# The state-space branch of a transformer kernel without GpSimd, and the attention's lambda at the very start

## The chip, the cores and the metric

The kernel runs on one core of a Trainium2 chip. A core has a matrix engine, TensorE (PE; its weight loads are listed apart as PEld), and three engines for elementwise work: VectorE (DVE), ScalarE (ACT) and GpSimd (POOL). Transfers are issued from the queues of SyncE (SP) or of another engine. Each engine takes its instructions in order, and waits on semaphores for the others. The metric is the device time of one execution in microseconds (us), as the median of several runs. In the profile L178 is line 178 of the kernel.

## The reference

One block over 512 tokens of width 1024: a state-space branch and a differential attention side by side, merged through gates, then cross attention to a memory, a feed-forward part, and two more layers with four branches each. The change touches only the first part:

```python
def s5_branch(u, lam_re, lam_im, log_dt, b_re, b_im, c_re, c_im, d_skip):
    ...
    lam_bar = jnp.exp(lam * dt)
    b_bar = ((lam_bar - 1.0) / lam)[..., None] * b
    bu = jnp.einsum('gph,blgh->lbgp', b_bar, ug)
    ...
    _, states = lax.associative_scan(combine, (a, bu), axis=0)
    y = jnp.einsum('ghp,lbgp->blgh', c, states).real
    y = y.reshape(bsz, seqlen, SSM_WIDTH) + d_skip.astype(F32) * u.astype(F32)
```

It has 64 groups of 16 channels with 64 complex states each. The differential attention (8 heads) subtracts a second softmax from a first, scaled by one number: lambda = exp(q1·k1) − exp(q2·k2) + a constant, from four learned vectors of 64 elements.

## The kernel before

**Matmuls.** Products in full precision are made from halves: each matrix is split into a rounded part and a remainder, and three matmuls are summed. A weight comes by transfer into a tile `raw`; ACT writes the rounded part `wh` (L177), DVE the remainder `wl` (L178); PE then runs `L1415` or `L272` matmuls of 128x512. Activations are split in the same way (`ap`, `qk`, `vv` and others).

**The mix stage.** `mix()` fills the first 480 us or so and is followed by cross attention, feed-forward and the other layers, which the change doesn't touch. It has four phases. (1) Four tiles of the input are normalised (`norm_tile`: ACT sums squares at L219, DVE makes the inverse root at L206 to L214, POOL or DVE scales at L296) and transposed. The first two weights of the state-space input are rounded by POOL (L1026). (2) The matmuls of u (`u_mm`, L272 and L1035), beside them `ssm_prep()`, which turns lambda and the step size into powers, and the first steps of the state-space generator. (3) The attention `da()`: per head and row block scores, softmax, the weights' combination (L894 to L897), output (L914), and a norm row (L925 to L928). A generator `fill()` puts the projections of later heads (`qk_in`, with the rotary step L960 to L967) and the gates between them. (4) The gated unit `glu()`, which reads the state-space output back from memory (`ysd`).

**The state-space generator.** `ssm_half(sp, hf, ...)` is run for two halves of 32 groups. It makes factors (L570 to L579) and a table of powers `apw` (L584 to L590); 16 pieces z of 128x512, three POOL instructions each (L608 to L610), which PE transposes (L614), ACT copies (L616) and PE multiplies with u (L623) into the state `E`; a scan in two levels of seven steps, k (L637 to L641) and b (L646 to L650), whose real part is on POOL and whose imaginary part is on DVE; then 16 pieces W of 128x576, again three POOL instructions each (L684 to L686), and the output (L717 to L741). Over both halves that makes 16 z and 16 W pieces. Each `yield` ends a step. In phase 2 the table `U_STEPS` sets how many steps follow each u tile; in phase 3 the attention earns a credit of 2.5 steps per turn (`SSM_RATE`).

**Order.** The kernel is written in the Tile framework: dependencies become semaphores, and a scheduler orders the instructions of each engine, starting from the order of the code.

**Lambda.** `da_lambda()` (L855 to L876) loads the four vectors into one partition of a tile `rp`, forms the two sums and exponentials on DVE (`exp_acc`, L411 to L423) and spreads the result over 128 partitions by a matmul with ones (L874). It is called after the last u matmul and before `fill()` begins:

```python
        p = self.psum("tp")
        nc.tensor.matmul(p[:, 0:2], z[0:1, 128:256], z[0:1, 16:18], start=True, stop=True)
        self.nlam = self.cst.tile([128, 1], F32, name="nlam")
        v.tensor_copy(self.nlam, p[:, 0:1])
```

Of the kernel before, what the change touches and what calls it, by code (L numbers as in the profile page):

```python
# [119 lines left out]
class Builder:  # L120
# [231 lines left out]
    def load_cols(self):  # L352
# [43 lines left out]
        nc.vector.tensor_scalar(self.half_glu, self.col("b_glu"), 0.5, None, op0=OP.mult)  # L396
        self.onesr = self.cst.tile([128, 1], F32R, name="onesr")
        nc.vector.tensor_scalar(self.onesr, self.ident[:, 0:1], 0.0, 1.0, op0=OP.mult, op1=OP.add)
# [61 lines left out]


    def ssm_prep(self, sp):
        nc, A, v = self.nc, self.A, self.nc.vector
        tl = lambda name, w: sp.tile([128, w], F32, name=name)
        k = [0]
# [11 lines left out]
        lr, li, dt, ld = new(), new(), new(), new()
        nc.sync.dma_start(lr, A["ssm_lambda_re"][0])
        nc.sync.dma_start(li, A["ssm_lambda_im"][0])
        nc.sync.dma_start(ld[:, 0:1], A["ssm_log_dt"][0].rearrange("(g o) -> g o", o=1))  # L480
        self.exp_acc(dt[:, 0:1], ld[:, 0:1], lambda: new()[:, 0:1])
# [55 lines left out]
        p1, p2 = tl("p1", 576), tl("p2", 576)  # L537
        v.tensor_copy(p1[0:64], pr[0:64])
        v.tensor_copy(p1[64:128], pi[64:128])
        v.tensor_copy(p2[0:64], pi[0:64])  # L540
        v.tensor_copy(p2[64:128], pr[64:128])
        self.P1, self.P2 = (x.rearrange("p (k g) -> p k g", k=9) for x in (p1, p2))
        asc = tl("asc", 128).rearrange("p (q f l) -> p q f l", q=4, f=8)
        for h in range(2):
            s = slice(h * 64, h * 64 + 64)
            for q, z in ((0, prv), (1, prv), (3, piv)):
                zz = z[s, 0].rearrange("p (f h l) -> p f h l", f=8, h=2)[:, :, h]
                v.tensor_copy(asc[s, q], zz)
        v.tensor_scalar(asc[:, 2], asc[:, 3], -1.0, None, op0=OP.mult)
        self.asc = asc.rearrange("p q f l -> p q (f l)")  # L550

    def ssm_half(self, sp, hf, us, ys, kd):
        nc, A, v, G = self.nc, self.A, self.nc.vector, self.nc.gpsimd
        g0 = hf * 32
# [14 lines left out]
        tmp = spg()  # L569
        G.tensor_mul(v3(B1), v3(U), bc(self.Frd))  # L570
        G.tensor_mul(v3(tmp), v3(V), bc(self.Fis))
        G.tensor_add(B1, B1, tmp)
        tmp = spg()
        G.tensor_mul(v3(X2), v3(V), bc(self.Frs))
        G.tensor_mul(v3(tmp), v3(U), bc(self.Fid))
        G.tensor_sub(X2, X2, tmp)
        v.tensor_copy(X1[0:64], B1[0:64])
        v.tensor_copy(X1[64:128], X2[64:128])
        v.tensor_copy(X2[64:128], B1[64:128])  # L579

        a = self.asc[:, :, hf * 16:hf * 16 + 16]
        ap = tl(384, "apw", 1).rearrange("p (q g k) -> p q g k", q=3, g=16)
        ct = self.small(64, "ct4", 1).rearrange("p (g k) -> p g k", g=16)
        v.tensor_copy(ap[:, 0, :, 0:1], a[:, 0, :, None])  # L584
        v.tensor_copy(ap[:, 1, :, 0:1], a[:, 3, :, None])
        for n in (1, 2, 4):
            m = ap[:, :, :, n - 1:n].to_broadcast([128, 3, 16, n])
            self.cmul(v, ap[:, 0, :, n:2 * n], ap[:, 1, :, n:2 * n], ap[:, 0, :, 0:n], ap[:, 1, :, 0:n],
                      m[:, 0], m[:, 1], ct[:, :, 0:n])
        v.tensor_scalar(ap[:, 2], ap[:, 1], -1.0, None, op0=OP.mult)  # L590
        yield
# [4 lines left out]
        for fl in range(4):  # L596
            u = self.page()
            nc.sync.dma_start(u, us[hf * 4 + fl])
            us_.append(u.rearrange("p (g c) -> p g c", g=8))
            Rs = []  # L600
            for h in range(2):
                gl = fl * 8 + h * 4
                z, t2 = spg(), spg()
                zv, tv = (x.rearrange("p (g k h) -> p g k h", g=4, k=8) for x in (z, t2))
                pw = lambda P: P[:, 1:9, g0 + gl:g0 + gl + 4].rearrange("p k g -> p g k")[
                    :, :, :, None].to_broadcast([128, 4, 8, 16])
                bw = lambda B: v3(B)[:, gl:gl + 4, None, :].to_broadcast([128, 4, 8, 16])
                G.tensor_mul(zv, pw(self.P1), bw(X1))  # L608
                G.tensor_mul(tv, pw(self.P2), bw(X2))
                G.tensor_add(z, z, t2)  # L610
                yield
                tp = self.psum("sx")
                for g in range(4):
                    nc.tensor.transpose(tp[:, g * 128:g * 128 + 128], z[:, g * 128:g * 128 + 128], self.ident)  # L614
                R = self.page()
                nc.scalar.activation(R, tp, AF.Copy)  # L616
                Rs.append(R)
                yield
            xp = self.psum("sx").rearrange("p (r l c) -> p r l c", r=2, l=4)
# [14 lines left out]
        for k in range(1, 8):  # L634
            pr = Eb[:, :, :, :, k - 1]
            for r, e in enumerate((G, v)):
                e.tensor_mul(m1[:, r], ab(0), pr[:, r])  # L637
                e.tensor_mul(m2[:, r], ab(2 + r), pr[:, 1 - r])
                e.tensor_add(m1[:, r], m1[:, r], m2[:, r])
            for r, e in enumerate((G, v)):  # L640
                e.tensor_add(Eb[:, r, :, :, k], Eb[:, r, :, :, k], m1[:, r])  # L641
            yield
        for b in range(1, 8):
            cr = lambda r: Eb[:, r, :, b - 1, 7:8].to_broadcast([128, 16, 8])
            for r, e in enumerate((G, v)):
                e.tensor_mul(m1[:, r], ap[:, 0], cr(r))  # L646
                e.tensor_mul(m2[:, r], ap[:, 2 - r], cr(1 - r))
                e.tensor_add(m1[:, r], m1[:, r], m2[:, r])
            for r, e in enumerate((G, v)):
                e.tensor_add(Eb[:, r, :, b, :], Eb[:, r, :, b, :], m1[:, r])  # L650
            yield
# [8 lines left out]
        for dst, key, sg in ((C1, "ssm_c_re", True), (C2, "ssm_c_im", False)):  # L660
# [5 lines left out]
            for f in range(4):  # L666
                nc.tensor.transpose(tp[:, f * 128:f * 128 + 128], ci[:, f * 128:f * 128 + 128], self.ident)
            if sg:
                v.tensor_scalar(dst, tp, self.sgn, -1.0, op0=OP.mult, op1=OP.mult)
            else:  # L670
                v.tensor_scalar(dst, tp, -1.0, None, op0=OP.mult)
            yield
# [3 lines left out]
        def kern(n):  # L676
# [175 lines left out]
    def da_lambda(self):  # L852
        nc, A, v = self.nc, self.A, self.nc.vector
        r = self.page(tag="rp")
        for j, n in enumerate(("da_lambda_q1", "da_lambda_k1", "da_lambda_q2", "da_lambda_k2")):  # L855
            nc.sync.dma_start(r[0:1, j * 64:j * 64 + 64], A[n])
        rv = r[0:1, 0:256].rearrange("p (a b n) -> p a b n", a=2, b=2)
# [12 lines left out]
        v.tensor_scalar(z[0:1, 16:17], z[0:1, 16:17], LAM_INIT, -1.0, op0=OP.add, op1=OP.mult)  # L870
        v.memset(z[0:1, 128:256], 1.0)
        v.tensor_copy(z[0:1, 17:18], z[0:1, 16:17])
        p = self.psum("tp")
        nc.tensor.matmul(p[:, 0:2], z[0:1, 128:256], z[0:1, 16:18], start=True, stop=True)  # L874
        self.nlam = self.cst.tile([128, 1], F32, name="nlam")
        v.tensor_copy(self.nlam, p[:, 0:1])  # L876

    def da(self, qk, need, vgen, yad, ssd, mask):
# [5 lines left out]
        def start(u):  # L884
# [37 lines left out]
        def norm(h, sq):  # L922
# [47 lines left out]
    def mix(self, stage=5):  # L970
# [82 lines left out]
        for f in range(8):  # L1053
# [962 lines left out]
```

## Time and profile before

| | |
|---|---|
| median of 3 runs | 2199.04 us (2193.31 to 2204.34) |
| the profiled execution | 2190.39 us |
| its span in the profile | 2188.4 us |
| mean granted PE clock | 0.979 |
| PE busy | 2094.1 us (96%) |
| DVE busy | 1301.3 us (59%) |
| ACT busy | 984.9 us (45%) |
| POOL busy | 350.6 us (16%) |

Busy times are sums over the whole span. The mix stage is about a fifth of it, and the shares there are others than these. The last matmul's end sets the end of the span, so the time that PE stands still, or runs at the lower clock, is what a change of the other engines can win or lose.

### The profile page before, as it was taken

What the parts mean: (1) busy time and instruction counts of PE and PEld (TensorE: products, weight loads), DVE (VectorE), ACT (ScalarE), POOL (GpSimd) and SP (SyncE); (2) the same over time, 40 slices, a digit from 0 to 9 for tenths busy, and PEclk for the clock granted to TensorE, in tenths of its full rate; (3) what the DMA queues carried; (4) which work ended last, traced back from release to release, by engine and by line L of the source; (5) the groups of instructions that cost most, each with busy time, mean ns of one, the idle gap of its engine ahead of it and who ended that gap; (6) DMA issues with size and microseconds to landing.
All of it is one profiled execution on the core that took longest, in us unless ns stands there. A gap on an engine that the chain in (4) does not pass through costs nothing.

```text
span 2188.4 us, 29605 instructions
## 1 busy us (share of the span) xinstructions
PE 2094.1 (96%) x11102; PEld 1729.9 (79%) x11102; DVE 1301.3 (59%) x2935; ACT 984.9 (45%) x1945; POOL 350.6 (16%) x310
## 2 busy tenths in 40 slices
PE   6798998989999999999999999999999999999998
PEld 6576776767788988888888887888888887888886
DVE  7788579655557556233336767674345667674344
ACT  5255664654247446342334645453234545453232
POOL 2676389400010000000001000001210000001210
PEclk8899999999999999999999999999999999999999
DMA  6424523445633331222233323232234323232321
GB/s 173 123 79 118 132 83 87 137 132 195 212 117 126 116 97 58 97 96 96 80 113 118 121 69 99 68 110 92 89 104 141 102 63 112 73 106 87 106 98 66
DMA packets 244614, 234.93 MB, mean 107 GB/s; under 512 B 56264, under 2 KB 198255, under 8 KB 244471
## 3 DMA queue, kind: packets, MB, share of 16 engines
q1 hardware_dynamic: 244470, 233.04, 34.5%
q8 instruction: 87, 1.43, 0.3%
q14 instruction: 57, 0.46, 0.1%
HBM read 212.01 MB, written 18.91 MB: 106 GB/s over the span
## 4 chain that ended last, share of the span: by engine, by line
PE 80%; DVE 10%; DMA 3%; ACT 3%; issue 2%; POOL 1%; SPq 0%; DVEq 0%; ACTq 0%; POOLq 0%
PE mm L1415 39%; PE mm L282 18%; PE mm L272 13%; DVE wl L178 2%; DMA rp<-rsd 1%; PE o L1681 1%; PE mm L1099 1%; PE sx L717 1%; PE at L842 1%; PE at L843 1%; DMA raw<-in_w_in 1%; PE o L1490 1%; ACT wh L177 1%; PE at L1291 1%; PE o L1329 1%
## 5 line engine op out<-in xcount | busy, mean ns | idle before, releaser
L178 DVE TENSOR_TENSOR wl<-raw,wh 128x1024 fp32r<-128x1024 f32 (+1 forms) x310 | 402.1, 1299 | 384.4 <-ACT wh L177 380.7
L177 ACT ACTIVATE wh<-raw 128x1024 fp32r<-128x1024 f32 (+1 forms) x310 | 332.3, 1074 | 466.9 <-PE mm L1415 177.4
L1415 PE MATMUL mm<-pg,wh 128*128 128x512 f32 (+1 forms) x896 | 276.4, 388 | 14.0 <-DVE rp L965 11.2
L1415 PE MATMUL mm<-qk,wh 128*128 128x512 f32 (+1 forms) x928 | 287.3, 390 | 2.4 <-ACT wh L177 1.7
L1415 PE MATMUL mm<-ap,wh 128*128 128x512 f32 (+1 forms) x928 | 288.1, 385 | 0.0
L282 PE MATMUL mm<-wh,pg 128*128 128x512 f32 x664 | 210.2, 391 | 0.3 <-ACT pg L177 0.3
L1887 POOL TENSOR_TENSOR pg<-pg,rp 128x512 f32<-128x512 f32 x48 | 68.7, 1430 | 865.7 <-DVE sum L1624 548.7
L1415 PEld LDWEIGHTS mm<-pg,wh 128*128 128x128 f32 x896 | 165.9, 193 | 48.2 <-DVE rp L965 13.0
L1415 PEld LDWEIGHTS mm<-qk,wh 128*128 128x128 f32 x928 | 173.0, 191 | 35.8 <-ACT wh L177 2.1
L1415 PEld LDWEIGHTS mm<-ap,wh 128*128 128x128 f32 x928 | 171.8, 188 | 32.8
L1415 PE MATMUL mm<-qk,wl 128*128 128x512 f32 (+1 forms) x464 | 180.3, 389 | 0.0
L1415 PE MATMUL mm<-ap,wl 128*128 128x512 f32 (+1 forms) x464 | 177.9, 384 | 0.0
L1415 PE MATMUL mm<-pg,wl 128*128 128x512 f32 (+1 forms) x448 | 173.8, 388 | 0.0
L282 PEld LDWEIGHTS mm<-wh,pg 128*128 128x128 f32 x664 | 124.2, 188 | 26.6 <-ACT pg L177 1.4
L282 PE MATMUL mm<-wl,pg 128*128 128x512 f32 x332 | 128.4, 390 | 0.0
L272 PE MATMUL mm<-ap,wh 128*128 128x512 f32 (+1 forms) x416 | 122.8, 378 | 1.5 <-DVE ivy L207 0.9
L272 PE MATMUL mm<-qk,wh 128*128 128x512 f32 (+1 forms) x416 | 121.8, 376 | 1.6 <-ACT qk L177 1.4
L1415 PEld LDWEIGHTS mm<-qk,wl 128*128 128x128 f32 x464 | 88.6, 191 | 17.1
L1383 POOL TENSOR_TENSOR pg<-pg,vv 128x512 f32<-128x512 f32 x8 | 10.5, 1323 | 565.0 <-ACT junk L219 559.6
L1415 PEld LDWEIGHTS mm<-pg,wl 128*128 128x128 f32 x448 | 86.1, 192 | 18.7 <-issue 3.0
L1415 PEld LDWEIGHTS mm<-ap,wl 128*128 128x128 f32 x464 | 87.2, 188 | 16.3
L272 PE MATMUL mm<-pg,wh 128*128 128x512 f32 (+1 forms) x320 | 88.0, 359 | 7.7 <-DVE pg L181 3.8
(564 smaller groups left out, 4037.4 us busy)
## 6 DMA issues: line engine op xcount, KB each, us to landing
raw<-in_w_in SPq DMA_DIRECT2D x70, 1024.0 KB
raw<-in_w_ff SPq DMA_DIRECT2D x32, 1024.0 KB
raw<-in_w_in SPq DMA_DIRECT2D x18, 512.0 KB
raw<-in_w_xkv SPq DMA_DIRECT2D x8, 1024.0 KB
raw<-in_w_branch SPq DMA_DIRECT2D x16, 512.0 KB
raw<-in_w_out SPq DMA_DIRECT2D x8, 1024.0 KB
gd<-rp SPq DMA_DIRECT2D x16, 256.0 KB
E<-kd SPq DMA_DIRECT2D x64, 64.0 KB
```

The costliest lines, as they stand in the source:

```text
L177: nc.scalar.activation(hi, src, AF.Copy)
L178: nc.vector.tensor_sub(lo, src, hi.bitcast(F32))
L272: self.nc.tensor.matmul(p, x[:, k, :], y[:, s], start=first and k == 0 and j == 0, stop=last and k == nk - 1 and j == 2)
L282: self.nc.tensor.matmul(p, x[:, s], y, start=k == 0 and j == 0, stop=k == nk - 1 and j == 2)
L717: nc.tensor.matmul(yp[HALF[h], g * 128:g * 128 + 128], x, y, start=g == 0 and c == 0, stop=g == 3 and c == 1, skip_group_check=True)
L842: mm(s, q[h][:, qs], hi, start=start, stop=False, skip_group_check=True)
L843: mm(s, q[h][:, qs], lo, start=False, stop=stop, skip_group_check=True)
L1099: nc.tensor.matmul(p[:, 0:256], x[:, s], y[:, k % 4, :], start=k == 0 and j == 0, stop=k == KT - 1 and j == 2)
L1291: nc.tensor.matmul(s[:, 0:256], x[:, sl], y, start=c == 0, stop=c == 5)
L1329: nc.tensor.matmul(o[:, 0:256], x[:, fs], y[:, m, :], start=c == 0, stop=c == 5)
L1415: self.nc.tensor.matmul(po, x[:, k, :], y[:, cols], start=c == 0, stop=c == 3 * nk - 1)
L1887: G.tensor_add(acc[m], acc[m], t)
```

## The change

All work of the state-space branch that was on POOL goes to DVE: the factors, the z and W products and the scan. A scan step becomes five DVE instructions of 128 or 256 columns for both parts together, and it yields twice where it yielded once. Copies that were on DVE go to ACT: the tables p1, p2 and asc, the factors' X1 and X2, the state E, the scaling of C, the norm rows of the attention, and the multiplication of a 128x1 column by lambda. The table apw is made once for both halves. `da_lambda()` and the loads of the state-space lambda are called ahead of the first norm, their loads are issued from ACT's queue, and lambda is spread by writing it to memory and reading it back into 128 partitions.

```diff
+    def ssm_loads(self):
+        nc, A = self.nc, self.A
+        t = self.ssm_in = self.page(tag="qk")
+        nc.scalar.dma_start(t[0:64, 0:64], A["ssm_lambda_re"][0])
+        nc.scalar.dma_start(t[0:64, 64:128], A["ssm_lambda_im"][0])
+        nc.scalar.dma_start(t[0:64, 128:129], A["ssm_log_dt"][0].rearrange("(g o) -> g o", o=1))
...
-        G.tensor_mul(v3(B1), v3(U), bc(self.Frd))
-        G.tensor_mul(v3(tmp), v3(V), bc(self.Fis))
-        G.tensor_add(B1, B1, tmp)
+        v.tensor_mul(v3(B1), v3(U), bc(self.Frd))
+        v.tensor_mul(v3(tmp), v3(V), bc(self.Fis))
+        v.tensor_add(B1, B1, tmp)
...
-        v.tensor_copy(X1[0:64], B1[0:64])
+        nc.scalar.activation(X1[0:64], B1[0:64], AF.Copy)
...
-                G.tensor_mul(zv, pw(self.P1), bw(X1))
-                G.tensor_mul(tv, pw(self.P2), bw(X2))
-                G.tensor_add(z, z, t2)
+                v.tensor_mul(zv, pw(self.P1), bw(X1))
+                v.tensor_mul(tv, pw(self.P2), bw(X2))
+                v.tensor_add(z, z, t2)
...
-            v.tensor_copy(Ev[:, :, fl * 4:fl * 4 + 4, :], xp)
+            nc.scalar.activation(Ev[:, :, fl * 4:fl * 4 + 4, :], xp, AF.Copy)
...
         for k in range(1, 8):
-            pr = Eb[:, :, :, :, k - 1]
-            for r, e in enumerate((G, v)):
-                e.tensor_mul(m1[:, r], ab(0), pr[:, r])
-                e.tensor_mul(m2[:, r], ab(2 + r), pr[:, 1 - r])
-                e.tensor_add(m1[:, r], m1[:, r], m2[:, r])
-            for r, e in enumerate((G, v)):
-                e.tensor_add(Eb[:, r, :, :, k], Eb[:, r, :, :, k], m1[:, r])
+            pr, to = Eb[:, :, :, :, k - 1], Eb[:, :, :, :, k]
+            v.tensor_mul(m1, a[:, 0:2, :, None].to_broadcast([128, 2, 16, 8]), pr)
+            for r in range(2):
+                v.tensor_mul(m2[:, r], ab(2 + r), pr[:, 1 - r])
+            v.tensor_add(m1, m1, m2)
+            v.tensor_add(to, to, m1)
+            yield
             yield
...
-            G.tensor_mul(Wv, pw(self.P1), bw(C1))
-            G.tensor_mul(tv, pw(self.P2), bw(C2))
-            G.tensor_add(W, W, t2)
+            v.tensor_mul(Wv, pw(self.P1), bw(C1))
+            v.tensor_mul(tv, pw(self.P2), bw(C2))
+            v.tensor_add(W, W, t2)
...
-            nc.sync.dma_start(r[0:1, j * 64:j * 64 + 64], A[n])
+            nc.scalar.dma_start(r[0:1, j * 64:j * 64 + 64], A[n])
...
-        v.memset(z[0:1, 128:256], 1.0)
-        v.tensor_copy(z[0:1, 17:18], z[0:1, 16:17])
-        p = self.psum("tp")
-        nc.tensor.matmul(p[:, 0:2], z[0:1, 128:256], z[0:1, 16:18], start=True, stop=True)
-        self.nlam = self.cst.tile([128, 1], F32, name="nlam")
-        v.tensor_copy(self.nlam, p[:, 0:1])
+        ld = self.dram.tile([1, 1], F32, name="nlamd")
+        self.nlam = self.cst.tile([128, 16], F32, name="nlam")[:, 0:1]
+        nc.sync.dma_start(ld, z[0:1, 16:17])
+        nc.sync.dma_start(self.nlam, ld[0, :].partition_broadcast(128))
...
-            v.tensor_mul(rs[:, 1:2], rs[:, 1:2], self.nlam)
+            nc.scalar.activation(rs[:, 1:2], rs[:, 1:2], AF.Copy, scale=self.nlam)
...
-            v.tensor_copy(r[0:1], p[0:1])
+            nc.scalar.activation(r[0:1], p[0:1], AF.Copy)
...
         v.tensor_copy(g_mix, p[:, 0:8])
+        self.da_lambda()
+        self.ssm_loads()
...
-        self.da_lambda()
```

PE's queue at the end of the u matmuls, before. `mm_1134` is the last u tile, `mm_1205` the first projection of the attention, `tp_1190` lambda's spreading:

```order
L272 MATMUL mm_1134<-pg_119,wh_1129 128x512
L272 MATMUL mm_1134<-pg_118,wl_1130 128x512
L1415 MATMUL mm_1205<-pg_104,wh_1197 128x512
L1415 MATMUL mm_1205<-pg_105,wh_1197 128x512
L874 MATMUL tp_1190<-rp_1167 128x2
L623 MATMUL sx_792<-pg_766,pg_778 64x64
L1415 MATMUL mm_1205<-pg_104,wl_1198 128x512
```

The same place on PE now, where the u tile is `mm_1146` and the first projection `mm_1184`:

```order
L272 MATMUL mm_1146<-pg_153,wh_1141 128x512
L631 MATMUL sx_826<-pg_800,pg_812 64x64
L272 MATMUL mm_1146<-pg_154,wh_1141 128x512
L272 MATMUL mm_1146<-pg_153,wl_1142 128x512
L1419 MATMUL mm_1184<-pg_139,wh_1176 128x512
L1419 MATMUL mm_1184<-pg_140,wh_1176 128x512
L1419 MATMUL mm_1184<-pg_139,wl_1177 128x512
```

The matmul of L874 is gone from between the projection's matmuls, and the first u products of the state-space branch (then L623, now L631) stand a few places earlier.

DVE's queue at the start, before: the column `gmix` of the first norm's weights, then the first tile's inverse root:

```order
L398 TENSOR_SCALAR onesr<-c_ident_76 128x1
L994 COPY gmix<-tp_100 128x8
L206 SCALAR_TENSOR_TENSOR ivx_123<-ss_120 128x1
L207 TENSOR_SCALAR ivy_124<-ivx_123 128x1
L208 TENSOR_TENSOR ivh_125<-ivy_124 128x1
```

DVE's queue at the same place now, from the first row of lambda on (`rp_104` holds the four vectors, `rp_110` the sums and exponentials):

```order
L864 TENSOR_TENSOR rp_104<-rp_104 1x128
L866 TENSOR_REDUCE rp_110<-rp_104 1x2
L411 TENSOR_SCALAR rp_110<-rp_110 1x2
L412 TENSOR_SCALAR rp_110<-rp_110 1x2
L413 TENSOR_SCALAR rp_110<-rp_110 1x2
L414 TENSOR_SCALAR rp_110<-rp_110 1x2
L415 SCALAR_TENSOR_TENSOR rp_110<-rp_110 1x2
L416 SCALAR_TENSOR_TENSOR rp_110<-rp_110 1x2
L418 TENSOR_SCALAR rp_110<-rp_110 1x2
L421 TENSOR_SCALAR rp_110<-rp_110 1x2
L420 SCALAR_TENSOR_TENSOR rp_110<-rp_110 1x2 x3
L206 SCALAR_TENSOR_TENSOR ivx_158<-ss_155 128x1
```

Eleven rows of lambda's work stand between `gmix` and the first inverse root; the rest of it follows between the rows of that root.

POOL's queue at the start, before: the scaling of the first norm tile, then the casts of the first two weights:

```order
L296 TENSOR_SCALAR rp_151<-ap_82,ivy_124 128x512
L1026 CAST wh_333<-raw_88 128x8x8x16
L1026 CAST wh_338<-raw_88 128x8x8x16
L296 TENSOR_SCALAR rp_197<-ap_86,ivy_170 128x512
L296 TENSOR_SCALAR rp_243<-ap_92,ivy_216 128x512
```

POOL's queue at the same place now:

```order
L1031 CAST wh_368<-raw_88 128x8x8x16
L1031 CAST wh_373<-raw_88 128x8x8x16
L296 ISA
L296 TENSOR_SCALAR rp_186<-ap_82,ivy_159 128x512
L296 TENSOR_SCALAR rp_232<-ap_86,ivy_205 128x512
```

The two casts stand ahead of the first norm tile's scaling, where they followed it.

## Rows read from the trace of the kernel before

**Rows 1.** The page, busy tenths in 40 slices of 54.7 us; PEclk is the granted clock.

```profile
POOL 2676389400010000000001000001210000001210
PEclk8899999999999999999999999999999999999999
```

**Rows 2.** Windows: length, busy PE, PEld, DVE, ACT, POOL (instructions); PEclk, DMA share, GB/s.

```profile
81.00:92.00 11.00, 0.09 (x1) 0.00 (x0) 10.73 (x35) 0.97 (x2) 6.34 (x5) 0.66 0.53 155
92.00:99.00 7.00, 6.89 (x46) 5.37 (x47) 1.59 (x4) 0.00 (x0) 0.00 (x0) 0.56 0.63 201
...
100.00:465.00 365.00, 339.30 (x2410) 265.78 (x2409) 272.58 (x576) 210.86 (x452) 221.77 (x217) 0.98 0.37 104
...
330.00:385.00 55.00, 47.56 (x222) 34.91 (x221) 51.61 (x102) 24.93 (x52) 49.57 (x60) 0.94 0.35 93
```

**Rows 3.** PE's waits from 100 to 482 us: us in total, times, longest.

```profile
PE mm L1415 <- DVE rp L965: 11.2, 4, 4.1
```

**Rows 4.** Timeline of PE and DVE, 68 to 93 us: start, duration, in brackets idle before.

```profile
69.14 1.22 DVE L178 TENSOR_TENSOR wl<-raw,wh 128x1024 fp32r<-128x1024 f32 x1
...
75.79 0.66 PE L614 MATMUL sx<-c_ident,sp 128*128 128x128 f32 x4 [3.09 <-POOL sp L610]
...
92.11 0.58 PE L874 MATMUL tp<-rp 1*128 1x2 f32 x2 [11.02 <-DVE rp L872]
```

**Rows 5.** Timeline of all engines, 84 to 87 us.

```profile
84.19 2.12 POOL L610 TENSOR_TENSOR sp<-sp,sp 128x512 f32<-128x512 f32 x1
85.12 1.22 DVE L411 TENSOR_SCALAR rp<-rp 1x2 f32<-1x2 f32 x1
...
86.26 0.15 DVE L412 TENSOR_SCALAR rp<-rp 1x2 f32<-1x2 f32 x1
```

**Rows 6.** Timeline of the start, DVE and the issues of SP (SPq).

```profile
6.47 0.16 DVE L206 SCALAR_TENSOR_TENSOR ivx<-ss 128x1 f32<-128x1 f32 x1 [3.16 <-ACT junk L219]
...
12.18 0.59 SPq L478 DMA_DIRECT2D qk<-in_ssm_lambda_re  x1
```

**Rows 7.** Timeline of DVE, 138 to 159 us, and L646 alone (ns: minimum, median, maximum).

```profile
138.29 0.27 DVE L639 TENSOR_TENSOR sp<-sp 128x128 f32<-128x128 f32 x1
138.49 1.59 DVE L178 TENSOR_TENSOR wl<-raw,wh 128x1024 fp32r<-128x1024 f32 x1
...
141.16 0.40 DVE L641 TENSOR_TENSOR E<-E,sp 128x128 f32<-128x128 f32 x1
141.47 0.39 DVE L638 TENSOR_TENSOR sp<-asc,E 128x128 f32<-128x128 f32 x1
...
158.05 0.68 DVE L967 TENSOR_TENSOR rp<-rp,rp 128x512 f32<-128x512 f32 x1
158.66 1.58 DVE L178 TENSOR_TENSOR wl<-raw,wh 128x1024 fp32r<-128x1024 f32 x1
...
L646 DVE TENSOR_TENSOR sp<-apw,E x14: 280/509/530, 171.9 to 375.2; 128x128 f32<-128x128 f32 x14
```

**Rows 8.** Groups of DVE to 500 us by form: us busy, mean ns, idle before.

```profile
L178 DVE TENSOR_TENSOR wl<-raw,wh 128x1024 fp32r<-128x1024 f32 x50 | 76.1, 1524 | 18.2 <-ACT wh L177 17.9
...
L895 DVE TENSOR_TENSOR rcp<-rcp,nlam 128x1 f32<-128x1 f32 x32 | 12.4, 387 | 0.6
L637 DVE TENSOR_TENSOR sp<-asc,E 128x128 f32<-128x128 f32 x14 | 10.9, 782 | 0.3
...
L650 DVE TENSOR_TENSOR E<-E,sp 128x128 f32<-128x128 f32 x14 | 6.2, 439 | 0.2
...
L626 DVE COPY E<-sx 128x512 f32<-128x512 f32 x8 | 5.5, 682 | 8.4 <-PE sx L623 8.4
```

**Rows 9.** Two kinds of ACT copies by line: ns minimum, median, maximum, first and last start.

```profile
L616 ACT ACTIVATE pg<-sx x16: 576/597/604, 76.5 to 319.4; 128x512 f32<-128x512 f32 x16
...
L1525 ACT ACTIVATE ct<-cx x4: 213/218/219, 1323.1 to 1818.1; 128x32 f32<-128x32 f32 x4
```

**Rows 10.** The chain of waits, 465 to 500 us.

```profile
474.49 5.87 DMA ex<-ysd
```

More of the change, by code (lines that the diff above doesn't have):

```diff
@@ L396, in load_cols @@
         nc.vector.tensor_scalar(self.half_glu, self.col("b_glu"), 0.5, None, op0=OP.mult)
-        self.onesr = self.cst.tile([128, 1], F32R, name="onesr")
+        self.onesr = self.cst.tile([128, 16], F32R, name="onesr")[:, 0:1]
         nc.vector.tensor_scalar(self.onesr, self.ident[:, 0:1], 0.0, 1.0, op0=OP.mult, op1=OP.add)
@@ L475, in new @@
             return tmp64()
[L477 to L480, printed above, removed]
+        lr, li, ld = (self.ssm_in[0:64, x * 64:x * 64 + 64] for x in range(3))
+        dt = new()
         self.exp_acc(dt[:, 0:1], ld[:, 0:1], lambda: new()[:, 0:1])
@@ L537, in ssm_prep @@
         p1, p2 = tl("p1", 576), tl("p2", 576)
[L538 to L541, printed above, removed]
+        for t, (x, y) in ((p1, (pr, pi)), (p2, (pi, pr))):
+            nc.scalar.activation(t[0:64], x[0:64], AF.Copy)
+            nc.scalar.activation(t[64:128], y[64:128], AF.Copy)
+        self.nsgn = tl("nsgn", 16)[:, 0:1]
+        v.tensor_scalar(self.nsgn, self.sgn, -1.0, None, op0=OP.mult)
         self.P1, self.P2 = (x.rearrange("p (k g) -> p k g", k=9) for x in (p1, p2))
@@ L547, in ssm_prep @@
                 zz = z[s, 0].rearrange("p (f h l) -> p f h l", f=8, h=2)[:, :, h]
-                v.tensor_copy(asc[s, q], zz)
+                nc.scalar.activation(asc[s, q], zz, AF.Copy)
         v.tensor_scalar(asc[:, 2], asc[:, 3], -1.0, None, op0=OP.mult)
-        self.asc = asc.rearrange("p q f l -> p q (f l)")
+        self.asc = a = asc.rearrange("p q f l -> p q (f l)")
+        self.apw = ap = tl("apw", 768).rearrange("p (q g k) -> p q g k", q=3, g=32)
+        ct = self.page(tag="rp")[:, 0:128].rearrange("p (g k) -> p g k", g=32)
+        v.tensor_copy(ap[:, 0, :, 0:1], a[:, 0, :, None])
+        v.tensor_copy(ap[:, 1, :, 0:1], a[:, 3, :, None])
+        for n in (1, 2, 4):
+            m = ap[:, :, :, n - 1:n].to_broadcast([128, 3, 32, n])
+            self.cmul(v, ap[:, 0, :, n:2 * n], ap[:, 1, :, n:2 * n], ap[:, 0, :, 0:n], ap[:, 1, :, 0:n],
+                      m[:, 0], m[:, 1], ct[:, :, 0:n])
+        v.tensor_scalar(ap[:, 2], ap[:, 1], -1.0, None, op0=OP.mult)
     def ssm_half(self, sp, hf, us, ys, kd):
-        nc, A, v, G = self.nc, self.A, self.nc.vector, self.nc.gpsimd
+        nc, A, v = self.nc, self.A, self.nc.vector
         g0 = hf * 32
@@ L569, in ssm_half @@
         tmp = spg()
-        G.tensor_mul(v3(B1), v3(U), bc(self.Frd))
-        G.tensor_mul(v3(tmp), v3(V), bc(self.Fis))
-        G.tensor_add(B1, B1, tmp)
+        v.tensor_mul(v3(B1), v3(U), bc(self.Frd))
+        v.tensor_mul(v3(tmp), v3(V), bc(self.Fis))
+        v.tensor_add(B1, B1, tmp)
         tmp = spg()
-        G.tensor_mul(v3(X2), v3(V), bc(self.Frs))
-        G.tensor_mul(v3(tmp), v3(U), bc(self.Fid))
-        G.tensor_sub(X2, X2, tmp)
-        v.tensor_copy(X1[0:64], B1[0:64])
-        v.tensor_copy(X1[64:128], X2[64:128])
-        v.tensor_copy(X2[64:128], B1[64:128])
-        a = self.asc[:, :, hf * 16:hf * 16 + 16]
[L582 to L590, printed above, removed]
+        v.tensor_mul(v3(X2), v3(V), bc(self.Frs))
+        v.tensor_mul(v3(tmp), v3(U), bc(self.Fid))
+        v.tensor_sub(X2, X2, tmp)
+        nc.scalar.activation(X1[0:64], B1[0:64], AF.Copy)
+        nc.scalar.activation(X1[64:128], X2[64:128], AF.Copy)
+        nc.scalar.activation(X2[64:128], B1[64:128], AF.Copy)
+        a = self.asc[:, :, hf * 16:hf * 16 + 16]
+        ap = self.apw[:, :, hf * 16:hf * 16 + 16]
         yield
@@ L634, in ssm_half @@
         for k in range(1, 8):
-            pr = Eb[:, :, :, :, k - 1]
-            for r, e in enumerate((G, v)):
-                e.tensor_mul(m1[:, r], ab(0), pr[:, r])
-                e.tensor_mul(m2[:, r], ab(2 + r), pr[:, 1 - r])
-                e.tensor_add(m1[:, r], m1[:, r], m2[:, r])
-            for r, e in enumerate((G, v)):
-                e.tensor_add(Eb[:, r, :, :, k], Eb[:, r, :, :, k], m1[:, r])
+            pr, to = Eb[:, :, :, :, k - 1], Eb[:, :, :, :, k]
[5 more added lines that the diff above has]
+            yield
             yield
         for b in range(1, 8):
[L644 to L650, printed above, removed]
+            cr, to = Eb[:, :, :, b - 1, 7:8], Eb[:, :, :, b, :]
+            v.tensor_mul(m1, ap[:, 0:1].to_broadcast([128, 2, 16, 8]), cr.to_broadcast([128, 2, 16, 8]))
+            for r in range(2):
+                v.tensor_mul(m2[:, r], ap[:, 2 - r], cr[:, 1 - r].to_broadcast([128, 16, 8]))
+            v.tensor_add(m1, m1, m2)
+            v.tensor_add(to, to, m1)
+            yield
             yield
@@ L667, in ssm_half @@
                 nc.tensor.transpose(tp[:, f * 128:f * 128 + 128], ci[:, f * 128:f * 128 + 128], self.ident)
[L668 to L671, printed above, removed]
+            nc.scalar.activation(dst, tp, AF.Copy, scale=self.nsgn if sg else -1.0)
             yield
```

## The prediction, made before the change was run

> **What bounds the kernel now.** I began with the page's slices of the span. GpSimd (POOL) does its work in the first ten and almost none later, and the granted clock of TensorE (PE) is below nine tenths only in the first two [rows 1]. The change touches nothing but the mix stage, which fills the first 482 us or so; behind it the instructions stand in the same order in both programs. So the whole question is how many microseconds PE loses in the mix stage, and how many of these the change gives back.
>
> Next, the stretches. From 81 to 92 us PE is busy for 0.09 us while VectorE (DVE) is busy for 10.73 of 11; from 92 to 99 us PE works, at a granted clock of 0.56, the lower of its two levels for most of it; from 100 to 465 us PE is busy for 339.3 of 365 us, so all that could still be won there is 25.7 us [rows 2]. Then PE's waits by what ended them: the largest group that is spread over the stage is 11.2 us in four waits for DVE's L965, a piece of the rotary step [rows 3]. The timeline has the two single ones: the transposes at 75.79 waited 3.09 us for POOL's products, and the matmul of L874 at 92.11, which spreads lambda over the partitions, waited 11.02 us for DVE [rows 4].
>
> Why was DVE late? The lambda chain is some twenty instructions on one or two elements. One of them took 1.22 us beside a POOL addition that itself took 2.12 us; the next, as POOL finished, took 0.15 us [rows 5]. Neither engine is itself slow there. They slow each other, and PE pays.
>
> **The change, part by part.**
>
> *Lambda.* The matmul goes; its result comes by a transfer long before the attention. The weights of the matmuls queued behind it were ready: the remainder of the first one was made at 69.14 [rows 4]. So the 11.0 us wait falls away whole, with the matmul's own 0.58 us [rows 4]: −11.6. With no idle stretch ahead of it, 92 to 99 us need not run at the lower clock: 6.89 us of PE work [rows 2] at full rate is 6.89 × 0.56 = 3.9 us, so −3.0.
>
> *Start.* The chain now stands on DVE ahead of the first norm, and seven transfers are issued by ScalarE (ACT) ahead of its first work. DVE is idle for 3.16 us before its first norm instruction at 6.47, which waits for ACT's sums of squares [rows 6]. Eleven rows of lambda work (thirteen instructions) now precede that instruction; at the unhindered 0.15 us of [rows 5] plus gaps they take about 2 us, and seven issues at SP's 0.59 us [rows 6] take 4.1 us, which ACT has while it waits for the input. The lambda transfers must land first, so the norms begin perhaps 1 us later. Against that, POOL's casts of the first weights now stand ahead of its part of the norms. I take 0, between −2 and +3; the new transfer lands unseen unless the attention gets there before it.
>
> *Products from POOL to DVE.* Undisturbed, DVE starts the next instruction 0.61 us after a 128x512 one (158.05 to 158.66), 0.31 us after a strided 128x128 one (141.16 to 141.47), 0.20 us after a contiguous one (138.29 to 138.49) [rows 7]. From these: 12 factor and 48 z instructions of 512 columns, 60 × 0.61 = 36.6 us; 48 W instructions of 576 columns, 48 × 0.61 × 576/512 = 32.9 us. A wider scan step follows from the two pairs: contiguous (0.61 − 0.20)/384 = 1.07 ns a column plus 0.06 us; strided, twice 0.31 less 0.06. A k step has two strided 256 (0.56 each), two strided 128 (0.31), one contiguous 256 (0.34): 2.1 us. A b step has three contiguous 256 and two contiguous 128: 1.4 us. Fourteen of each: 49 us. Added: about 119 us.
>
> *Leaving DVE.* Its half of the scan, eight groups of 14, of which [rows 8] show the dearest and the cheapest: 14 × 8 × (0.782 + 0.439)/2 = 68 us by their mean. The copies: 12.4 us in L895, 5.5 us in the eight of E [rows 8], and 28 others (X, p, asc, C, the norm rows) at about the same 0.6 to 0.7 us: 35 in all. Removed: about 103 us. By count DVE gains 16 us of work. But it no longer shares with POOL: the 50 weight remainders of L178 have a mean of 1524 ns in the stage [rows 8], the one at 69.14 took 1.22 us [rows 4], so 50 × 0.30 = 15 us come back there alone, and others profit as well. DVE's total in the stage comes out level, or up to 25 us lower.
>
> *Waiting on z.* DVE makes a piece in 3 × 0.61 = 1.8 us, the first before PE gets there, as its place in DVE's queue is ahead of the second attention weight. The wait at 75.79 goes: −3.1.
>
> *Copies to ACT.* A 128x512 copy takes 597 ns there, a small scaling 218 ns [rows 9]: 32 × 0.22 + about 36 × 0.5 = 25 us more for ACT, which is busy for 210.86 of the 365 us [rows 2]. That room hides it; without it the copies would delay the weight splits that ACT makes, by up to those 25 us.
>
> *The rest.* The 25.7 us of idle PE between 100 and 465 us [rows 2] stem from DVE being late (the L965 waits), scan stretches above all: from 330 to 385 us DVE is busy for 51.61 of 55 us and PE loses 7.4 [rows 2]. DVE level in work but undisturbed should ease the four L965 waits by about a third: −4. The bounds are −15, if most of that idle time goes, and +12, if the 25 us of copies on ACT and the 16 us on DVE surface by a third.
>
> Sum: −11.6 − 3.0 − 3.1 + 0 − 4 = −22, rounded. The profiled execution took 2190.4 us, so 2168; the median of the runs shown is 8.7 us above it, so the forecast for the median is **2177 us**.
>
> **The rivals.**
>
> *More comes back (2165).* In the scan and W stretches DVE is as crowded as the stage gets. If that is all the mutual slowing of [rows 5], the rest of the lower bound comes too, 11 to 12 us: 2177 − 12 = 2165, down to 2158 if the start gains as well. For it: the 1524 against 1226 ns. Against: 16 us more DVE work by count, and W products that now delay softmax work in the same queue.
>
> *Given back (2195).* PE arrives 18 us earlier at each place, but what it then needs is late by the same amount: weights by transfer, or the reload of the state-space output before the gated unit. At the end of the stage the chain of waits holds such a reload, of 5.87 us [rows 10]. An earlier PE waits longer there unless the scan, which now spends two turns of the weaving per step, ends as much earlier. If all 18 us of the named waits return, 2177 + 18 = 2195. Against: transfers use 0.37 of their engines from 100 to 465 us [rows 2].
>
> *DVE becomes the bound (2210).* The products read repeated columns and stepped places, and these could cost DVE what strided steps do: 0.31 − 0.20 over 128 columns is 0.86 ns a column. That makes 8 × 0.44 on factors, 32 × 0.44 on z and 32 × 0.495 on W, 33 us more. If all of it lay on PE's path, 2177 + 33 = 2210; from two thirds on, the gain is gone. Against: L646, whose second operand repeats, has a minimum of 280 ns, and a contiguous 128x128 at 138.29 took 0.27 us [rows 7], so repeating seems free.
>
> The Trainium skill, page "Vector Engine (DVE) Microarchitecture Reference", section "5.2 Measured stream behaviour on trn2 (trn3 not measured)", speaks for this rival: an operand that hops at every element streams at 1.73 ns a column in place of 1.05, while adjacent pairs cost nothing. By its figures the 72 multiplies would cost about 26 us more, an estimate, and the forecast would be 2203 if all were exposed. By that rule the trace agrees on the strided scan, where 0.31 stands against 0.20 us; that a repeated word counts as a hop the L646 row denies [rows 7].
>
> *It does nothing at the wait.* PE loses the 11.0 us to whichever DVE result is next in the queue. I count this with the given-back case, as the time is the same.
>
> **How the numbers follow.** Forecast (2168 to 2187) 0.52; more comes back 0.22; given back 0.17; DVE the bound 0.09. About 0.5%, 11 us, is what a measurement of this kernel can tell from no change, so 2188 to 2210 counts as the same. The first two cases are faster, 0.74; given back is the same, 0.17; the last is slower, 0.09. The range of 2158 to 2197 takes in the first three cases but for their tails; the forecast's own is 2168 to 2187.
>
> **What would show it.** Right: no PE wait near 80 to 92 us, full clock behind it, the attention's first scores some 20 us earlier than before, weight remainders of a mean near 1.25 us, z multiplies near 0.6 us on DVE. Wrong: DVE multiplies with repeats near 1 us; PE waits of several us for ACT's weight splits; waits for the ysd reload that grow by what was gained; a first matmul more than 3 us late.

## The result and the profile after

The changed kernel took 2164.14 us (median of 4 runs, 2161.81 to 2168.11), the kernel before 2197.11 us: a ratio of 0.985, 95% interval 0.9823 to 0.9876, or 33 us less. The forecast was 2177. The profiled execution took 2161.81 us with a span of 2160.0, 28.4 us under that of before, whose profiled execution (2190.39 us) lay 6.7 us below that median.

The page's slices of 54 us, as in [rows 1]:

```profile
POOL 2000000000100000000001000001210000001210
PEclk9998999999999999999999999999999999999999
```

The windows, columns as in [rows 2]:

```profile
81.00:92.00 11.00, 11.00 (x79) 8.85 (x78) 5.42 (x11) 3.03 (x6) 0.00 (x0) 1.00 0.95 272
92.00:99.00 7.00, 5.98 (x54) 4.82 (x53) 6.01 (x8) 4.99 (x9) 1.27 (x1) 1.00 0.15 52
```

The hole from 81 to 92 us is filled, and the clock behind it is whole. Where each part of the time came from is read from five places on PE's timeline. Before: first u matmul, first attention projection, first scores, start of the gated unit, first matmul behind it:

```profile
13.80 0.36 PE L272 MATMUL mm<-pg,wh 128*128 128x256 f32 x1 [1.39 <-ACT pg L180]
...
80.47 0.62 PE L1415 MATMUL mm<-pg,wh 128*128 128x512 f32 x2
...
118.20 0.33 PE L814 MATMUL at<-qk,qk 64*128 64x128 f32 x2
...
470.31 0.73 PE L1415 MATMUL mm<-ex,wh 128*128 128x512 f32 x2 [0.45 <-ACT ex L180]
...
536.88 0.72 PE L272 MATMUL mm<-pg,wh 128*128 128x512 f32 x2 [1.49 <-ACT rp L1125]
```

The same places after:

```profile
17.33 0.55 PE L272 MATMUL mm<-pg,wh 128*128 128x256 f32 x1 [0.70 <-ACT pg L180]
...
80.01 0.62 PE L1419 MATMUL mm<-pg,wh 128*128 128x512 f32 x2
...
104.08 0.33 PE L819 MATMUL at<-qk,qk 64*128 64x128 f32 x2
...
447.94 0.73 PE L1419 MATMUL mm<-ex,wh 128*128 128x512 f32 x2 [2.07 <-ACT ex L180]
...
509.36 0.72 PE L272 MATMUL mm<-pg,wh 128*128 128x512 f32 x2 [1.50 <-ACT rp L1129]
```

So the start lost 3.5 us; the u matmuls won 4.0 (no wait for z); up to the first scores came 13.7; the attention to the gated unit gave 8.2, the gated unit 5.1, and all behind it 0.9. The gated unit ends at 537 us before, so the stage is longer than the 480 us or so given for it above. Its windows and those of the attention, before and then after, columns as in [rows 2]:

```profile
118.20:470.31 352.11, 325.19 (x2310) 253.69 (x2309) 264.78 (x570) 203.12 (x442) 206.43 (x205) 0.98 0.39 107
470.31:536.88 66.57, 56.51 (x222) 42.75 (x222) 33.55 (x69) 29.30 (x53) 0.00 (x0) 0.90 0.53 170
...
104.08:447.94 343.86, 325.00 (x2311) 254.16 (x2310) 261.83 (x609) 222.64 (x492) 20.25 (x14) 0.97 0.40 111
447.94:509.36 61.42, 51.80 (x222) 40.12 (x222) 32.55 (x65) 30.23 (x55) 0.00 (x0) 0.97 0.57 185
```

In the attention PE is as busy as before (325 us) and stands still for 18.9 us in place of 26.9, with DVE's busy time level. In the gated unit it stands still nearly as long (9.6 against 10.1 us): 4.7 of the 5.1 us are shorter busy time, at a granted clock of 0.97 in place of 0.90.

DVE's groups by form to 472 us, as in [rows 8], with one z multiply by line (ns: minimum, median, maximum):

```profile
L178 DVE TENSOR_TENSOR wl<-raw,wh 128x1024 fp32r<-128x1024 f32 x50 | 66.4, 1329 | 27.7 <-ACT wh L177 27.6
L968 DVE TENSOR_TENSOR rp<-mm,pg 128x512 f32<-128x512 f32 x16 | 11.0, 688 | 8.1 <-ACT rp L967 7.9
L970 DVE TENSOR_TENSOR rp<-rp,rp 128x512 f32<-128x512 f32 x16 | 10.9, 681 | 1.0 <-POOL rp L969 1.0
...
L617 DVE TENSOR_TENSOR sp<-p,X x16: 674/683/691, 69.6 to 291.5; 128x512 f32<-128x512 f32 x16
```

Repeated columns cost nothing that shows: the z multiply's 683 ns is that of L970 without repeats. The weight remainders fell from 1524 [rows 8] to 1329 ns. The mean mixes two layouts: six of the 50 belong to weights of u, whose elements are rearranged as they are split, and take 2.0 to 2.2 us in the changed kernel even where POOL does nothing (from 34.7 to 94.1 us), as in the first line below. With the other 44 at 1.22 us that alone makes a mean of about 1.33. From 100 to 440 us, where POOL is nearly idle, none is slow any more (second line after, third before):

```profile
49.66 2.19 DVE L178 TENSOR_TENSOR wl<-raw,wh 128x1024 fp32r<-128x1024 f32 x1 [2.88 <-ACT wh L177]
...
L178 DVE TENSOR_TENSOR wl<-raw,wh x37: 1204/1222/1240, 105.0 to 438.1; 128x1024 fp32r<-128x1024 f32 x37
...
L178 DVE TENSOR_TENSOR wl<-raw,wh x36: 1202/1226/2195, 103.2 to 433.1; 128x1024 fp32r<-128x1024 f32 x36
```

PE's waits from 50 to 500 us no longer name DVE's rotary step ([rows 3]). The largest are now for ACT: for its rounding of the reloaded state-space output, and for the copy of the norm row, which the change moved to ACT (first two lines). Before, the same two cost 7.4 and 0.8 us (last two):

```profile
PE mm L1419 <- ACT ex L180: 9.2, 4, 3.1
PE tp L951 <- ACT ya L930: 5.4, 3, 2.6
...
PE mm L1415 <- ACT ex L180: 7.4, 4, 3.6
PE tp L948 <- DVE ya L927: 0.8, 1, 0.8
```

### The profile page after: what moved, and what is told of

Its sections match the earlier page's. It is cut to its first block, busy times and chain, and to the rows that moved or that the text cites. A ratio compares the mean times of both kernels' runs of the same rounds, so it can differ in the third digit from the quotient of the medians.

```text
span 2160.0 us, 29476 instructions
## 1 busy us (share of the span) xinstructions
PE 2081.7 (96%) x11100; PEld 1725.6 (80%) x11100; DVE 1289.3 (60%) x2980; ACT 1011.7 (47%) x2013; POOL 127.7 (6%) x90
## 4 chain that ended last, share of the span: by engine, by line
PE 83%; DVE 8%; DMA 4%; ACT 3%; issue 1%; SPq 1%; DVEq 0%; ACTq 0%
PE mm L1419 41%; PE mm L282 18%; PE mm L272 12%; PE mm L1103 2%; DMA rp<-rsd 2%; DVE wl L178 1%; PE o L1685 1%; PE sx L722 1%; PE at L847 1%; DMA raw<-in_w_in 1%; PE at L819 1%; PE at L848 1%; PE o L1494 1%; PE o L917 1%; PE at L1295 1%
## 5 line engine op out<-in xcount | busy, mean ns | idle before, releaser
L178 DVE TENSOR_TENSOR wl<-raw,wh 128x1024 fp32r<-128x1024 f32 (+1 forms) x310 | 393.1, 1270 | 392.9 <-ACT wh L177 388.0
L1419 PEld LDWEIGHTS mm<-ap,wh 128*128 128x128 f32 x928 | 171.8, 188 | 32.6
L272 PEld LDWEIGHTS mm<-ap,wh 128*128 128x128 f32 x416 | 77.1, 190 | 16.6 <-ACT ap L180 1.3
```

Source lines behind the costliest of these rows:

```text
L178: nc.vector.tensor_sub(lo, src, hi.bitcast(F32))
L272: self.nc.tensor.matmul(p, x[:, k, :], y[:, s], start=first and k == 0 and j == 0, stop=last and k == nk - 1 and j == 2)
L1419: self.nc.tensor.matmul(po, x[:, k, :], y[:, cols], start=c == 0, stop=c == 3 * nk - 1)
```

## The experiments

All are set against the kernel before (2196 to 2197 us in each group) and compared with the changed kernel's 2164. The theory to be tested: DVE was late because POOL worked beside it. The rivals: lambda's place alone; DVE's amount of work; waits for POOL's results.

**Lambda back (lam_late).**

```diff
-        self.da_lambda()
         self.ssm_loads()
...
                 next(sm)
+        self.da_lambda()    # with the old code: loads on SP, matmul
```

> The changed kernel, but lambda is computed and spread as in the kernel before: loads on SP, matmul on TensorE, called after the u matmuls. Theory (the 11 us wait came from DVE and GpSimd slowing each other): with GpSimd idle the chain's small instructions take about 0.15 us each and TensorE waits under 3 us for the spread; the start is no longer late by 3.5 us; about 2161 us (2156 to 2167). Rival (the chain's place in DVE's queue made the wait, whoever shares): the wait of some 11 us and the half clock behind it return, about 2164 + 14 - 3 = 2175 us.

2162.6 us, ratio 0.9848 (0.9833 to 0.9863): no slower than the changed kernel. The first and the last instruction of the chain on DVE, and the spreading matmul on PE; then the first and last of the chain in the kernel before:

```profile
90.69 0.28 DVE L864 TENSOR_TENSOR rp<-rp 1x128 f32<-1x128 f32 x1 [2.55 <-DMA rp<-in_da_lambda_k]
105.49 0.14 DVE L877 COPY rp<-rp 1x1 f32<-1x1 f32 x1
106.03 0.38 PE L879 MATMUL tp<-rp 1*128 1x2 f32 x2
...
79.51 1.24 DVE L859 TENSOR_TENSOR rp<-rp 1x128 f32<-1x128 f32 x1
91.91 0.14 DVE L872 COPY rp<-rp 1x1 f32<-1x1 f32 x1
```

With POOL's work on DVE the move of lambda is worth nothing measurable. But the reason isn't a faster chain: one instruction takes 0.15 us (L412 at 93.33), yet from first to last it takes 14.8 us, against 12.4 in the kernel before, as DVE's other work stands between them. PE doesn't wait because the scheduler now puts the matmul at 106 us, behind the first scores (105.22), and no longer ahead of the projections. Whether a quiet POOL alone would have ended the wait at the old place was not tested. That the start would be on time was wrong: the first u matmul came at 18.84 us. In its trace `ssm_prep()`, whose loads are still early, has instructions on DVE between those of the second norm tile's inverse root, and PE waits 3.98 us for that tile's scaling.

**Only lambda moved (lam_only).** The kernel before with the new `da_lambda()` and its call at the start, nothing else.

> The kernel before, with only lambda moved to the start and spread by a transfer. Theory (lambda is about half of the gain, the end of the mutual slowing the other half): 13 to 15 us won at the wait, 3.5 lost at the start, about 2186 us (2181 to 2191). Rival (lambda is the whole gain): 2164 to 2170 us. Rival (DVE is late there anyway, and TensorE waits for the next thing): 2195 to 2200 us.

2186.71 us, ratio 0.9959 (0.9943 to 0.9974): 10 us, as the theory had it. In the profiled execution the first scores come 6.0 us earlier than before, but the gated unit only 0.1 us; this execution (2186.63 us) is 3.8 us faster than the profiled one of before, so the 10 us are of the medians alone:

```profile
112.19 0.33 PE L814 MATMUL at<-qk,qk 64*128 64x128 f32 x2
...
470.21 0.74 PE L1413 MATMUL mm<-ex,wh 128*128 128x512 f32 x2 [0.45 <-ACT ex L180]
```

The waits on POOL and on the rotary step stay, in PE's waits to 482 us:

```profile
PE mm L1413 <- DVE rp L963: 11.5, 4, 4.4
...
PE sx L614 <- POOL sp L610: 4.4, 1, 4.4
```

**Products back on POOL (pool_products), and the scan (pool_scan).** Two kernels, each with one of these edits and lambda and the copies as changed:

```diff
-                v.tensor_mul(zv, pw(self.P1), bw(X1))
+                G.tensor_mul(zv, pw(self.P1), bw(X1))    # and the other factor, z and W lines
```

```diff
-            v.tensor_mul(m1, a[:, 0:2, :, None].to_broadcast([128, 2, 16, 8]), pr)
+            for r, e in enumerate((G, v)):               # and the rest of the old loops, one yield
+                e.tensor_mul(m1[:, r], ab(0), pr[:, r])
```

> The changed kernel with the factors and the z and W products back on GpSimd; the scan stays on DVE. Theory (GpSimd working beside DVE slows both more than DVE gains by 70 us less work): weight remainders back to a mean of 1.45 us or more, waits for z and for the rotary step return, 2172 to 2180 us. Rival (DVE's load counts, not the sharing): DVE is freer by 70 us, 2155 to 2164 us.

> The changed kernel with the scan shared between GpSimd and DVE again as in the kernel before (one yield per step, too). Theory (sharing costs): DVE has some 20 us less of its own work but is slowed, 2168 to 2176 us. Rival (load counts): 2156 to 2164 us.

2172.81 us (ratio 0.989, 0.9874 to 0.9907) and 2181.9 us (0.9935, 0.9919 to 0.9951): 9 and 18 us slower than the changed kernel, with less work on DVE. In the first the rotary wait and the slow remainders are back (PE's waits, DVE's groups); a wait for z hardly is (0.3 us). One wait of 9.0 us, ending at 338, is as long as the whole loss, and DVE's queue ahead of it shows the cause: two scan instructions that take 0.70 us together at 318.89, where POOL is idle, take 2.91 beside its W products:

```profile
PE mm L1419 <- DVE rp L968: 12.0, 4, 9.0
...
L178 DVE TENSOR_TENSOR wl<-raw,wh 128x1024 fp32r<-128x1024 f32 x50 | 77.5, 1553 | 27.7 <-ACT wh L177 22.2 <-PE mm L1419 5.4
...
318.89 0.70 DVE L646 TENSOR_TENSOR sp<-asc,E 128x128 f32<-128x128 f32 x2
...
333.96 1.60 POOL L690 TENSOR_TENSOR W<-p,X 128x576 f32<-128x576 f32 x1
...
334.40 2.91 DVE L646 TENSOR_TENSOR sp<-asc,E 128x128 f32<-128x128 f32 x2
...
337.97 1.22 PE L1419 MATMUL mm<-pg,wh 128*128 128x512 f32 x2 [9.04 <-DVE rp L968]
```

To the end of the gated unit DVE is busy for 368.3 us against 377.4 in the changed kernel, though about 80 us of its work have gone to POOL.

The second was slower than expected. Its remainders are only at 1366 ns, so sharing may not be all of it; each shared step also passes through POOL, where L646 takes a mean of 883 ns against 399 on DVE in the changed kernel. The two parts were not separated.

**POOL work for nothing (pool_spare, pool_spare_1).** The changed kernel with n = 3 or n = 1 extra POOL multiplications behind each transposed z piece and each of two copies of an output piece:

```diff
                 nc.scalar.activation(R, tp, AF.Copy)
+                for _ in range(n):
+                    G.tensor_mul(self.spare, R[:, 0:448], R[:, 0:448])
```

> The changed kernel with 96 extra GpSimd multiplications of 448 columns into a tile that nobody reads, three behind each transposed z piece and each output piece; nothing is left out. Theory (GpSimd slows DVE by working, not by being waited for): DVE's weight remainders rise above a mean of 1.40 us, 4 to 10 us slower than the changed kernel, 2168 to 2174 us. Rival (only waits for GpSimd's results cost): 2162 to 2166 us.

> The changed kernel with 32 extra GpSimd multiplications that nobody reads, one where the earlier experiment had three; nothing is left out. Theory (each GpSimd instruction costs DVE some time, so the loss follows their number): a third of the 21 us, 2169 to 2173 us. Rival (the loss came from the queue or from another order of instructions, not from the amount): either near 2164 or near 2185 us.

2185.12 us (ratio 0.9954, 0.9938 to 0.997) with 96 and 2166.15 us (0.9864, 0.9839 to 0.9888) with 32: 21 us, and 2. Both expectations on the amount failed: more than was thought with 96, less with 32. Windows up to the first matmul behind the gated unit, columns as in [rows 2], of the changed kernel, with 32, with 96:

```profile
0.00:509.36 509.36, 457.62 (x3033) 363.91 (x3033) 377.42 (x951) 311.05 (x654) 36.60 (x26) 0.98 0.46 131
...
0.00:512.47 512.47, 462.71 (x3032) 366.63 (x3033) 390.88 (x951) 310.34 (x654) 78.95 (x58) 0.97 0.46 130
...
0.00:534.12 534.12, 469.28 (x3033) 371.67 (x3033) 415.29 (x951) 310.31 (x654) 149.65 (x122) 0.95 0.44 125
```

POOL's busy time rose by 42 and 113 us, DVE's by 13.5 and 37.9, for the same 951 instructions: about a third of a us for each. DVE's loss does follow the amount. The run's time doesn't: the first 13.5 us of it cost 2, the next 24 cost 19. The remainders' mean with 96 is 1373 ns, under the 1.40 us expected. One reserve: the extra work also holds tiles. With 96, four DVE instructions at the output pieces waited 3.3 us in all for it, since they overwrite what it reads, and loads on SP 4.3 us. How much of the 21 us comes by that way was not separated. Which instructions are hit shows in two neighbours of the rotary step with 96 extra multiplications:

```profile
L977 DVE TENSOR_TENSOR rp<-rp,rp 128x512 f32<-128x512 f32 x16 | 15.9, 991 | 0.6 <-POOL rp L976 0.5
...
L975 DVE TENSOR_TENSOR rp<-mm,pg 128x512 f32<-128x512 f32 x16 | 11.0, 688 | 7.0 <-ACT rp L974 4.2 <-PE tp L935 2.5
```

The one that reads a matmul's result (`mm`) and one other tile keeps its 688 ns; the one with both inputs in ordinary tiles goes from 681 to 991. The Trainium skill says so on its page "GPSIMD Engine Reference", section "8. Key points": GpSimd shares its memory interfaces with VectorE, and VectorE instructions with two inputs there contend. The traces agree: 991 against 688 ns.

**Copies back on DVE (copies_dve).** `v.tensor_copy` and `v.tensor_mul` in place of the `nc.scalar.activation` copies.

> The changed kernel with the copies back on DVE: p1, p2, asc, X1, X2, E, the scaling of C, the norm rows and the multiplication by lambda. Theory (DVE is the late engine, ACT has room): 30 us more on DVE cost 3 to 10 us, 2167 to 2174 us. Rival (neither engine is short once GpSimd is quiet): 2162 to 2166 us. Rival (the copies on ACT delay weight splits): below 2160 us.

2168.5 us, ratio 0.9868 (0.9848 to 0.9889). The interval overlaps that of the changed kernel; this doesn't tell the theories apart.

**One yield per scan step (one_yield).** One of the two `yield` lines removed.

> The changed kernel with one yield per scan step, as before the change. Theory (the second yield spreads a longer chain of DVE steps, at no great price): 2162 to 2169 us. Rival (the spread is what keeps the scan from delaying the attention): over 2172 us.

2166.62 us, ratio 0.986 (0.984 to 0.988, overlapping): the second yield is worth nothing that can be told.

**Lambda behind the norms (after_norms).**

```diff
-        self.da_lambda()
-        self.ssm_loads()
         hT = self.new_T()
         for t in range(NT):
             self.norm_tile(xs[t], hT, t, g_mix, first=True)
+        self.da_lambda()     # all their loads on nc.sync
+        self.ssm_loads()
```

> The changed kernel, but lambda and its loads, and the loads of the state-space lambda, stand after the four norm tiles in the program and are issued by SP. Theory (the early lambda delays the first matmul by 3.5 us and this is kept to the end): first u matmul at about 13.8 in place of 17.3 us, 3 to 4 us faster than the changed kernel, 2160 us. Rival (the lateness is absorbed by later waits): 2164 us, no difference.

2162.08 us, ratio 0.9839 (0.9823 to 0.9855): not told from 2164. Its profiled execution took 2166.25 us, 4 us above its median. Its first u matmul comes at 14.84. First scores, start of the gated unit and first matmul behind it, then the window of the gated unit, and those from the first u matmul to the first scores of this kernel and of the changed one:

```profile
99.00 0.33 PE L819 MATMUL at<-qk,qk 64*128 64x128 f32 x2
...
446.43 0.73 PE L1419 MATMUL mm<-ex,wh 128*128 128x512 f32 x2 [2.07 <-ACT ex L180]
...
510.23 0.72 PE L272 MATMUL mm<-pg,wh 128*128 128x512 f32 x2 [1.50 <-ACT rp L1129]
...
446.43:510.23 63.80, 55.41 (x222) 42.85 (x222) 32.54 (x65) 30.19 (x55) 0.00 (x0) 0.89 0.56 176
...
14.84:99.00 84.16, 77.78 (x472) 65.93 (x472) 76.36 (x250) 49.01 (x86) 7.53 (x6) 0.98 0.59 156
...
17.33:104.08 86.75, 78.35 (x494) 67.99 (x494) 74.23 (x213) 49.71 (x87) 11.02 (x6) 1.00 0.57 147
```

The scores come 5.1 us earlier than in the changed kernel, but with 22 fewer matmuls ahead of them (472 against 494), so a part of this is order and no lead. The gated unit starts 1.5 us earlier and ends 0.9 later: PE is busy there for 55.4 us at a granted clock of 0.89, against 51.8 at 0.97. Why the clock was lower there is not shown.

**A faster weaving (norms_rate3), the rotary step off POOL (rope_dve), and with lambda behind the norms (norms_rope).** `SSM_RATE = 3.0` on after_norms; `v.tensor_mul(sw, sw, sin)` in place of POOL's.

> The kernel with lambda behind the norms, and the state-space generator woven in at 3.0 steps per turn in place of 2.5. Theory (the 5 us won at the start are given back where the gated unit waits for the reload of the state-space output, as that output is not ready earlier): the reload waits at the end of the stage fall from about 8 us to under 3, 2156 to 2159 us. Rival (the lead is lost in the scan stretches or at weights): 2161 to 2166 us, as the crowding there grows with the rate.

> The changed kernel with the last GpSimd work of the attention, one multiplication of the rotary step (16 in all), on DVE too. Theory (sharing costs both): 10 us more DVE work, 22 us less GpSimd work beside it, weight remainders under a mean of 1.30 us, 2158 to 2163 us. Rival (DVE's load counts by now): 2165 to 2172 us.

> The kernel with lambda behind the norms and the rotary multiplication on DVE. Theory (both small gains hold): 2155 to 2161 us. Rival (a lead before the end of the stage is given back at the reload of the state-space output): 2161 to 2165 us, as with either alone.

2163.54 us (0.9851, 0.9825 to 0.9876), 2162.33 us (0.9843, 0.9821 to 0.9866) and 2162.86 us (0.9842, 0.982 to 0.9865). None is told from the changed kernel. The faster weaving left the reload waits at 8.4 us, so that theory of where the lead goes was not borne out. Without the rotary step on POOL the remainders stayed at 1331 ns, not under 1.30 us: the six of u don't depend on POOL. No version tried beats the changed kernel measurably.

## Why the prediction was right, and where its steps were not

The sign held, and the range, which was 39 us wide, and the time is that of the case "more comes back" (2165). The likeliest case, 2168 to 2187, was missed by 4 us. Of the 13 us between forecast and measurement, 6.4 lie in the stages (28.4 us in place of 22), the others in the 8.7 us that the forecast added from the profiled execution to the median: after the change that distance is 2.3. By its steps:

- **Lambda, −14.6.** Measured to the first scores: −13.7. But the matmul's place in PE's queue, ahead of the projections, was a cause beside the mutual slowing. Moved alone, lambda gave 10 us; left late, with POOL's work on DVE, it costs nothing, as its matmul then stands behind the first scores. The two gains don't add.
- **Waiting on z, −3.1.** Measured: −4.0 up to the first projection.
- **Start, 0 (−2 to +3).** Measured: +3.5, just outside its bounds, and one of the prediction's signs of being wrong. The step counted the issues on ACT as hidden in ACT's wait and left out that SP issues beside them. SP's issues of the second four pieces of the input, before, in after_norms and after, and ACT's first work on them after:

```profile
3.88 2.38 SPq L330 DMA_DIRECT2D ap<-in_x  x4
...
3.89 3.50 SPq L330 DMA_DIRECT2D ap<-in_x  x4
...
5.22 3.52 SPq L330 DMA_DIRECT2D ap<-in_x  x4
...
12.90 0.63 ACT L219 ACTIVATE junk<-ap 128x512 bf16<-128x512 f32 x1 [3.66 <-DMA ap<-in_x]
```

  The second four start late after the change, and ACT waits for them to 12.90 with the scaling of the first tile (13.53; 8.76 before) queued behind. The late start goes with the issues on ACT: 5.03 to 5.62 us in the eight kernels with seven of them, 3.87 to 3.90 in the four with none. The longer issue does not: after_norms has none and takes 3.50. By after_norms the time lost there doesn't measurably reach the end.
- **The rest, −4 (−15 to +12).** This is the term that was mis-sized: 8.2 + 5.1 = 13.3 us from the first scores to the end of the gated unit, inside its bounds. The prediction valued the end of the mutual slowing as a third of the rotary waits; all 11.2 us of them went, and a part came back as waits for ACT. The 5.1 us are mostly the granted clock of the gated unit, which the sum counted only behind lambda's wait. The rival "more comes back" had the amount.
- **The remainders, 15 us.** Measured: 76.1 to 66.4, 9.7 us. The step took all 50 down to 1.22 us; the six of u stay at 2.0 to 2.2. DVE's total to the end of the gated unit fell from 390.0 to 377.4 us, within "level, or up to 25 us lower".
- **DVE becomes the bound.** Refuted by 683 ns for a multiply with repeats. The rule that the prediction cites from the Trainium skill (page "Vector Engine (DVE) Microarchitecture Reference", section "5.2 Measured stream behaviour on trn2 (trn3 not measured)") is on operands that hop at every element; its table has no row for a repeated word, and here the repeat cost nothing.
- **Given back.** Not in the size that the rival had: in the changed kernel the reload waits grew only from 7.4 to 9.2 us. In the traces the lead of lam_only, 6.0 us at the first scores, is 0.1 at the gated unit; but the medians of the same two kernels differ by 10 us, so that this lead is lost is not settled.

What stays open: how much of pool_scan's 18 us is sharing and how much POOL's slower steps; whether a quiet POOL without another order of PE's queue would have ended lambda's wait; and what sets the granted clock in the gated unit, where the profiled executions differ most.

## What to carry to other kernels

Work on GpSimd isn't free because its result isn't waited for: ask which VectorE instructions with two inputs in ordinary memory run beside it. A wait that can be removed in two ways is to be counted once. A lead that TensorE wins early need not last (in one pair of traces 6.0 us at the scores, 0.1 at the gated unit), so value a saving by whole runs. A mean over one line can mix layouts: look at its members before taking the fastest as what all can reach.

## What the runs showed of the hardware that was not expected

Each microsecond of the extra GpSimd work added about a third of a us to VectorE's busy time (13.5 for 42, 37.9 for 113), though nobody read its result. Of two neighbours of 128x512, the one with both inputs in ordinary tiles went from 681 to 991 ns, the one that reads a matmul's result kept its 688 ns.
